# Two groups of weight parts, an earlier modulation region and moved down blocks in a hybrid backbone block

## The chip, the cores and the metric

The kernel runs on one core of a Trainium2 chip. A core has a matrix engine (TensorE, "PE" in the profile, with its weight loads as "PEld"), a vector engine (DVE), a scalar engine (ACT), GpSimd (POOL), and SyncE (SP), which here only issues DMAs. TensorE writes to eight accumulation banks (PSUM); everything else works on the on-chip memory (SBUF). The metric is the device time of one execution in microseconds (us); lower is better.

## The reference, cut to what matters

One layer of a backbone for 512 latent tokens (8 rows of 64) and 256 context tokens, model width 2048, all in f32. First a mixer, then an MLP:

```python
mod = (c_act @ w_mod + b_mod)
sh1, sc1, gt1, sh2, sc2, gt2 = jnp.split(mod, 6, axis=-1)
h = rmsnorm(x, g_norm1) * (1 + sc1) + sh1
...                                   # 4 GLA heads and 4 mLSTM heads, both directions
x = x + gt1 * merge_groups(...)       # gates, per-head norm, output projection w_out
h2 = rmsnorm(x, g_norm2) * (1 + sc2) + sh2
x = x + gt2 * conv_ffn(h2, rows, GRID_W, w_up, conv_w, conv_b, w_down)
return rmsnorm(x, g_final)

def conv_ffn(h, rows, cols, w_up, conv_w, conv_b, w_down):
    u = h @ w_up
    u_gate, u_val = jnp.split(u, 2, axis=-1)            # 5504 columns each
    g = conv3x3_depthwise(u_gate on the 8 x 64 grid) + conv_b
    return (jax.nn.silu(g) * u_val) @ w_down
```

The six modulation regions sh1 to gt2 each are 2048 sums over 2048 inputs. The last one, gt2 (region 5), scales the MLP's output.

## The kernel before, in words

Activations lie transposed, features on the 128 partitions and tokens along the free axis. Each f32 matmul is made of three in a faster 32-bit format (`fp32r`): an operand is split in a high part (a cast on ACT, line 91) and a low part (the difference, on DVE, line 92), and `mm3` (L106) adds high x high, high x low, low x high. So every weight block goes through DMA to a `raw` buffer, an ACT cast to `hi` and a DVE subtraction to `lo`, in `load_split` (L176). The pools of these three are in `wts`.

Order of work: head projections (`project_steps`, L357), woven into the scans of the head before; gates (`w_gates`), output projection (`w_out`), second norm, then the MLP in 11 units of features: unit 0 has 3 blocks of 128 features, the ten others 4 each (43 in all). A unit is: gate half of the up-projection (`up_gate`, tiles `ug`), 3x3 convolution on ACT and DVE (`convolve`), value half (`up_val`, tiles `uv`), products `gh`/`gl`, and the down-projection in four blocks of 512 outputs (`down_sums`, tiles `dn`), which in the program stand one unit later, between the gate half and the value half of the next unit. Their results go from the banks through ACT to `st` tiles and by POOL's accumulating DMAs to `dacc` in HBM (units 0 to 8) or, scaled by region 5, to `x2d` (later ones). `fold` (L1265) scales `dacc` once and adds it to `x2d`, in unit 9.

The up-projections of units 1 to 10 use a 2 x 2 block scheme with seven products (`seven`, L1153) in place of eight: of a weight block of 512 columns and a token block of two k-rows, quarter sums are formed. The token sums are made once (`token_sums`, `token_last`, tiles `bq` and `bt`). The weight sums are made on DVE for every block by `load_sums` (L186): a `raw` tile of 7 x 256 columns takes the 4 loaded quarters and 3 sums written beside and over them, and then all 1792 columns are cast and subtracted as one part. `four` (L1165) combines the seven banks.

Modulation regions 2 to 5 are no matmuls: a chunk (`mod_chunk`, L283) loads 512 KB of `w_mod` and adds two scaled halves to a sum tile on DVE; 8 chunks make a quarter of a region, then four small matmuls with ones and one more on TensorE end it (`mod_sums`, `mod_end`; TensorE keeps these in written order). Chunks are a list of "fillers"; each `load_split` or `load_sums` calls `fill`, which takes `rate[0]` of them on average. Before: regions 2, 3, 4 fill the mLSTM heads' projections (rate 2 from the fourth step on), the gates and the output projection (rate 1.5); region 5 fills the down blocks of units 0 to 7 (rate 0.7), and its chunks take their buffers from the MLP's own `raw` pool (three buffers). In the heads, a chunk's buffer is one of the scan's tiles `sc` and `qi`.

A planner at build time orders the instructions of each engine and gives out buffers: by program order, with blocks in `high_priority` first, and with an instruction held back while its buffer is still in use by a modelled time. Where `pinned` is set, TensorE keeps the written order. A tile pool with tags gives each tag its own buffers; `yp` has sixteen 128 x 512 tiles, `y0` to `y15` (`ytile`), which hold x, then the MLP's convolutions and products. Before the MLP the banks are two pools, `psA` (six, tag `acc`) and `psB` (two); `st_p.close()` (L1114) ends them and one pool of eight takes their place. The broadcast of the second norm's statistics is in a bank of `psB`, read by L1109 for all 16 blocks of x.

Of the kernel before, what the change touches and what calls it, by code (L numbers as in the profile page):

```python
# [18 lines left out]
P = 128  # L19
# [52 lines left out]
def block_kernel(ctx: ExitStack, tc: tile.TileContext, a: dict, out: bass.AP):  # L72
# [102 lines left out]

    def load_split(src, name, n=2, w=512):  # L176
        raw = wts[0].tile([P, n, w], F32, name=f"raw_{name}", tag="raw")
        hi = wts[1].tile([P, n, w], F32R, name=f"hi_{name}", tag="hi")
        lo = wts[2].tile([P, n, w], F32R, name=f"lo_{name}", tag="lo")
        nc.sync.dma_start(raw, src)  # L180
        with tc.high_priority():
            parted[0] = split(hi, lo, raw)
        fill()
        return hi, lo

    def load_sums(src, name):  # L186

        x = wts[0].tile([P, 7, HW], F32, name=f"raw_{name}", tag="raw")
        hi = wts[1].tile([P, 7, HW], F32R, name=f"hi_{name}", tag="hi")
        lo = wts[2].tile([P, 7, HW], F32R, name=f"lo_{name}", tag="lo")  # L190
        nc.sync.dma_start(x[:, 0:4, :], src.rearrange("p a (b c) -> p (a b) c", c=HW))
        with tc.high_priority():
            add(x[:, 4:6, :], x[:, 0:4:3, :], x[:, 1:2, :].to_broadcast([P, 2, HW]))
            add(x[:, 6, :], x[:, 5, :], x[:, 0, :])
            add(x[:, 1, :], x[:, 2, :], x[:, 6, :])
            split(hi, lo, x)
        fill()
        return hi, lo
# [747 lines left out]
    mod_fillers((2, 3, 4))  # L946
# [60 lines left out]
    rate[0] = 1.5  # L1007
# [74 lines left out]
    pinned[0] = False  # L1082
    assert not fillers
# [5 lines left out]
    wts[:] = [pool(ctx, "mraw", 3, waits="tile"), pool(ctx, "mhi", 2, waits="tile"), pool(ctx, "mlo", 2, waits="tile")]  # L1089
# [3 lines left out]
    mod_raw.append(wts[0])  # L1093
    rate[0] = 0

# [17 lines left out]

    st_p.close()  # L1114
    banks8.append(pool(ctx, "psM", 8, PSUM, waits="tile"))
# [29 lines left out]
    def sum_tile(i, name):  # L1145
        return ytile(15, f"sum{i}_{name}") if i else fp.tile([P, T], F32, name=f"sum{i}_{name}", tag="sum0")


    mod_fillers((5,))

    PRODUCTS = ((0, bq, 0), (2, bq, 2), (6, bt, 2), (4, bt, 1), (5, bt, 0), (1, bq, 3), (3, bq, 1))

    def seven(src, name):  # L1153

        ps = [acc(f"{name}_{n}", (P, 2, HW)) for n in range(7)]
        for kp in range(KP):
            wh, wl = load_sums(src[kp], f"{name}_{kp}")
# [278 lines left out]
```

## Time and profile before

| | |
|---|---|
| median of 3 runs | 2653.06 us (2650.87 to 2656.63) |
| profiled execution | 2654.82 us, its span 2653.1 us |
| TensorE busy | 2513.1 us (95%), mean granted clock 0.984 |
| DVE, ACT, POOL busy | 68%, 37%, 8% |
| data moved | 380.56 MB, mean 143 GB/s |
| gates and output projection | about 762 to 1138 us of the span |
| MLP, units 0 to 10 | about 1146 to 2644 us |

Times in the trace are in us from the span's start. A line of a group or of the timeline has the program line, the engine, the operation, `out<-in` by tile names, shapes, the count, then the time; in brackets or behind a bar stands how long the engine had been idle just before, and what ended that idle time. A line of a stretch has its bounds and length, then busy time (and count) of PE, PEld, DVE, ACT and POOL, the granted TensorE clock as a share of full speed, the mean busy share of the 16 DMA engines and GB/s. Matmuls overlap their successors, so the step from one to the next is shorter than a matmul's own time.

### The profile page before, as it was taken

The numbers are of one execution on the slowest core, as the hardware profiler recorded it, in microseconds if no ns is written. First come the engines' busy times: TensorE is split into PE (matmuls) and PEld (weight loads), VectorE is DVE, ScalarE is ACT, GpSimd is POOL, SyncE is SP. The second block draws the span as 40 slices with busy tenths as digits, with TensorE's granted clock in tenths as the row PEclk, the third lists the DMA queues.
The fourth block names the chain that finished last, engine by engine and source line by source line (L and its number), as shares of the span: only waits on it lengthen the run. The fifth ranks groups of instructions, "written<-read, shape, count | busy, mean of one in ns | idle before, by whom it ended". The sixth has DMA issues, their size and how long they took to land.

```text
span 2653.1 us, 38849 instructions
## 1 busy us (share of the span) xinstructions
PE 2513.1 (95%) x15740; PEld 2230.2 (84%) x15740; DVE 1805.1 (68%) x2720; ACT 993.5 (37%) x1370; POOL 200.3 (8%) x274
## 2 busy tenths in 40 slices
PE   6999999999999999979998999999999999997997
PEld 4887899898888888868897989797988898987886
DVE  6657655454457576378887777777787777774866
ACT  4225543322222332254434343333433334343434
POOL 0000000000000000000102020101010101013021
PEclk9999999999999999989999999999999999999999
DMA  9740011132256686223537373736373645469473
GB/s 380 273 144 31 27 49 48 64 127 90 89 180 220 213 277 218 98 70 108 187 104 184 98 180 99 177 110 168 118 183 110 162 121 140 118 142 205 126 198 103
DMA packets 124108, 380.56 MB, mean 143 GB/s; under 512 B 14420, under 2 KB 18840, under 8 KB 123928
## 3 DMA queue, kind: packets, MB, share of 16 engines
q1 hardware_dynamic: 94680, 318.29, 35.9%
q0 software_dynamic: 28160, 58.73, 12.1%
q8 instruction: 123, 2.02, 0.3%
q10 hardware_dynamic: 1088, 1.05, 0.1%
q14 instruction: 57, 0.47, 0.1%
HBM read 323.49 MB, written 54.53 MB: 142 GB/s over the span
## 4 chain that ended last, share of the span: by engine, by line
PE 67%; DVE 14%; DMA 10%; issue 7%; POOL 1%; ACT 1%; SPq 0%; DVEq 0%; POOLq 0%; ACTq 0%
PE a L97 18%; PE uv L97 12%; PE ug L97 10%; PE ga L97 7%; PE wo L97 7%; PE dn L97 4%; DMA raw_m<-in_w_mod 4%; PE po L97 3%; DMA raw_uv<-in_w_up 3%; DVE cv L1208 2%; DVE lo_ug L92 2%; DVE lo_d L92 2%; DVE raw_ug L88 1%; PE sl L97 1%; PE ps_m L97 1%
## 5 line engine op out<-in xcount | busy, mean ns | idle before, releaser
L97 PE MATMUL dn<-gh,lo_d 128*128 128x512 f32 x672 | 266.0, 396 | 19.8 <-DVE lo_d L92 19.7
L97 PE MATMUL dn<-gh,hi_d 128*128 128x512 f32 x672 | 265.1, 395 | 5.1 <-ACT gh L91 5.1
L97 PE MATMUL dn<-gl,hi_d 128*128 128x512 f32 x672 | 264.4, 393 | 0.0
L1208 DVE SCALAR_TENSOR_TENSOR cv<-pads,cwt,cv 128x512 f32<-128x512 f32 x344 | 240.1, 749 | 2.2 <-ACT cv L1206 1.6
L97 PE MATMUL uv<-bqh,lo_uv 128*128 128x256 f32 (+1 forms) x688 | 205.1, 299 | 32.8 <-DVE lo_uv L92 32.7
L92 DVE TENSOR_TENSOR lo_uv<-raw_uv,hi_uv 128x1792 fp32r<-128x1792 f32 (+1 forms) x88 | 169.2, 1926 | 96.6 <-ACT hi_uv L91 96.5
L97 PE MATMUL ug<-bqh,hi_ug 128*128 128x256 f32 (+1 forms) x688 | 201.1, 296 | 31.5 <-DVE x L1109 17.8
L91 ACT CAST hi_uv<-raw_uv 128x1792 fp32r<-128x1792 f32 (+1 forms) x88 | 141.7, 1610 | 233.0 <-PE uv L97 198.2
L92 DVE TENSOR_TENSOR lo_ug<-raw_ug,hi_ug 128x1792 fp32r<-128x1792 f32 (+1 forms) x88 | 168.7, 1925 | 74.2 <-ACT hi_ug L91 74.1
L97 PE MATMUL uv<-bqh,hi_uv 128*128 128x256 f32 (+1 forms) x688 | 203.2, 295 | 6.6 <-ACT hi_uv L91 6.6
L91 ACT CAST hi_ug<-raw_ug 128x1792 fp32r<-128x1792 f32 (+1 forms) x88 | 140.9, 1612 | 169.3 <-PE ug L97 110.9
L97 PE MATMUL uv<-bql,hi_uv 128*128 128x256 f32 (+1 forms) x688 | 202.7, 295 | 0.0
L97 PE MATMUL ug<-bqh,lo_ug 128*128 128x256 f32 (+1 forms) x688 | 197.8, 298 | 5.0 <-DVE lo_ug L92 4.9
L298 DVE SCALAR_TENSOR_TENSOR sum_m<-raw_m,csil,sum_m 128x512 f32<-128x512 f32 x240 | 180.0, 750 | 31.4 <-DMA raw_m<-in_w_mod 26.8
L97 PE MATMUL ug<-bql,hi_ug 128*128 128x256 f32 (+1 forms) x688 | 197.9, 291 | 0.0
L88 DVE TENSOR_TENSOR raw_uv<-raw_uv 128x256 f32<-128x256 f32 (+1 forms) x240 | 121.7, 512 | 96.8 <-DMA raw_uv<-in_w_up 93.2
L1263 POOL DMA_DIRECT2D dacc<-st x128 | 111.9, 923 | 964.8 <-ACT st L1259 964.3
L97 PEld LDWEIGHTS dn<-gh,lo_d 128*128 128x128 f32 x672 | 127.7, 190 | 52.9 <-DVE lo_d L92 26.5
L97 PEld LDWEIGHTS uv<-bqh,lo_uv 128*128 128x128 f32 x688 | 134.5, 196 | 38.1 <-DVE lo_uv L92 36.2
L97 PEld LDWEIGHTS ug<-bqh,hi_ug 128*128 128x128 f32 x688 | 132.5, 193 | 37.6 <-issue 21.6
L97 PEld LDWEIGHTS dn<-gh,hi_d 128*128 128x128 f32 x672 | 127.7, 190 | 31.7 <-ACT gh L91 5.3
L97 PE MATMUL a<-hi_h,hTh 128*128 128x256 f32 x512 | 150.5, 294 | 0.5 <-ACT e L391 0.5
(349 smaller groups left out, 6811.6 us busy)
## 6 DMA issues: line engine op xcount, KB each, us to landing
raw_m<-in_w_mod SPq DMA_DIRECT2D x192, 512.0 KB, 5.0
raw_d<-in_w_down SPq DMA_DIRECT2D x82, 512.0 KB, 3.8
raw_ug<-in_w_up SPq DMA_DIRECT2D x80, 512.0 KB, 3.5
raw_uv<-in_w_up SPq DMA_DIRECT2D x80, 512.0 KB, 5.3
dacc<-st POOLq DMA_DIRECT2D x144, 256.0 KB, 5.5
raw_h<-in_w_heads SPq DMA_DIRECT2D x64, 512.0 KB, 3.5
raw_ga<-in_w_gates SPq DMA_DIRECT2D x32, 512.0 KB, 3.5
raw_wo<-in_w_out SPq DMA_DIRECT2D x32, 512.0 KB, 3.6
```

What stands on the lines that cost most here:

```text
L88: V.tensor_tensor(out=o, in0=x, in1=y, op=ALU.add)
L91: S.copy(hi, x)
L92: return V.tensor_tensor(out=lo, in0=x, in1=hi.bitcast(F32), op=ALU.subtract).ins
L97: ins = PE.matmul(*args, **kw)
L298: V.scalar_tensor_tensor(out=parts[0], in0=x, scalar=ck, in1=parts[0], op0=ALU.mult, op1=ALU.add)
L1208: V.scalar_tensor_tensor(out=t3, in0=src, scalar=w, in1=t3, op0=ALU.mult, op1=ALU.add)
L1263: nc.gpsimd.dma_start(x2d[k] if q > FOLD else dacc[k], t, accum_op=ALU.add)
```

## The change

Four things are edited.

1. `load_sums` no longer makes one part of seven quarters. The host orders each block's quarters as 0, 2, 3, 1. The first three are split as they are, in buffers of their own (`ahi`, `alo`, two each); three additions on DVE write four sums to a separate tile (`msum`, two), which is split in the buffers that down weights use too (`mhi`, `mlo`, two each). `raw` has four buffers of 4 KB a partition instead of three of 7 KB. The seven products are reordered so that the three plain ones come first, and `four` follows.
2. Region 5 joins regions 2 to 4 ahead of the MLP. Head 4's projection, woven into the last GLA head's scan, gets fillers as well (10 chunks), and the rate in gates and output projection goes from 1.5 to 2. The MLP has none.
3. The gate half of unit 0 is traced ahead of `st_p.close()`, so it accumulates in `psA`.
4. Unit 0: token sums of pairs 7 to 3 go ahead of the value half, the others and `token_last` behind it; its tiles take other places in `yp`; two of its down blocks go ahead of unit 1, the first of them feature by feature. The fourth down block of unit 9 goes behind the value half of unit 10, the last four blocks of x are fetched later, and some tiles of the end change places.

```diff
+    def split_new(x, name, shape, at=1):
+        hi = wts[at].tile([P, *shape], F32R, name=f"hi_{name}", tag=f"hi{at}")
+        lo = wts[at + 1].tile([P, *shape], F32R, name=f"lo_{name}", tag=f"lo{at}")
+        parted[0] = split(hi, lo, x)
+        return hi, lo
...
     def load_sums(src, name):
-        x = wts[0].tile([P, 7, HW], F32, name=f"raw_{name}", tag="raw")
-        hi = wts[1].tile([P, 7, HW], F32R, name=f"hi_{name}", tag="hi")
-        lo = wts[2].tile([P, 7, HW], F32R, name=f"lo_{name}", tag="lo")
-        nc.sync.dma_start(x[:, 0:4, :], src.rearrange("p a (b c) -> p (a b) c", c=HW))
+        x = load_raw(src, name).rearrange("p a (b c) -> p (a b) c", c=HW)
+        s = wts[5].tile([P, 4, HW], F32, name=f"sum_{name}", tag="sum")
         with tc.high_priority():
-            add(x[:, 4:6, :], x[:, 0:4:3, :], x[:, 1:2, :].to_broadcast([P, 2, HW]))
-            add(x[:, 6, :], x[:, 5, :], x[:, 0, :])
-            add(x[:, 1, :], x[:, 2, :], x[:, 6, :])
-            split(hi, lo, x)
-        fill()
-        return hi, lo
+            plain = split_new(x[:, 0:3, :], f"a{name}", (3, HW), 3)
+            add(s[:, 0:2, :], x[:, 0:3:2, :], x[:, 3:4, :].to_broadcast([P, 2, HW]))
+            add(s[:, 2, :], s[:, 1, :], x[:, 0, :])
+            add(s[:, 3, :], s[:, 2, :], x[:, 1, :])
+            sums = split_new(s, f"b{name}", (4, HW))
+        return plain, sums
...
-            rate[0] = 2 if h > H and kp >= 3 else 0
+            rate[0] = 2 if h >= H and kp >= 3 else 0
...
-    mod_fillers((2, 3, 4))
+    mod_fillers((2, 3, 4, 5))
...
-    rate[0] = 1.5
+    rate[0] = 2.0
...
-    wts[:] = [pool(ctx, "mraw", 3, waits="tile"), pool(ctx, "mhi", 2, waits="tile"), pool(ctx, "mlo", 2, waits="tile")]
+    wts[:] = [pool(ctx, n, b, waits="tile")
+              for n, b in (("mraw", 4), ("mhi", 2), ("mlo", 2), ("ahi", 2), ("alo", 2), ("msum", 2))]
...
-    st_p.close()
-    banks8.append(pool(ctx, "psM", 8, PSUM, waits="tile"))
...
-    mod_fillers((5,))
-    PRODUCTS = ((0, bq, 0), (2, bq, 2), (6, bt, 2), (4, bt, 1), (5, bt, 0), (1, bq, 3), (3, bq, 1))
+    PRODUCTS = ((0, 0, bq, 0), (0, 1, bq, 2), (0, 2, bq, 1), (1, 2, bt, 2), (1, 0, bt, 1), (1, 1, bt, 0), (1, 3, bq, 3))
...
+            put(1, 0, v, p4, ALU.subtract)
             put(1, 1, v, p5, ALU.add)
             sub(u, u, p5)
             put(0, 1, u, p3, ALU.add)
-            put(1, 0, v, p4, ALU.subtract)
...
-            t = ytile(8 + 2 * i, f"cv{f}")
+            t = ytile(8 + i if q == 0 else 8 + 2 * i, f"cv{f}")
...
-    for q in range(NQ):
+    up_gate(0)
+    st_p.close()
+    banks8.append(pool(ctx, "psM", 8, PSUM, waits="tile"))
+    for j in reversed(range(3, KP)):
+        token_sums(j)
+    up_val(0, convolve(0))
+    for j in range(3):
+        token_sums(j)
+    for j in range(KP):
+        token_last(j)
+    down_sums(0, (0, 1), True)
+    for q in range(1, NQ):
         up_gate(q)
-        if q == 0:
-            for j in range(KP):
-                token_sums(j)
-        if q:
-            rate[0] = 0.7 if q < FOLD + 1 else 0
-            down_sums(q - 1)
-            rate[0] = 0
+        down_sums(q - 1, (2, 3) if q == 1 else range(3) if q == NQ - 1 else range(4))
         if q - 1 == FOLD:
             fold()
         up_val(q, convolve(q))
-        if q == 0:
-            with tc.high_priority():
-                for j in range(KP):
-                    token_last(j)
+    down_sums(NQ - 2, (3,))
...
-    for k in range(KT):
+    for k in range(12):
         nc.gpsimd.dma_start(x2[k], x2d[k])
...
+        if blk == 0:
+            for k in range(12, KT):
+                nc.gpsimd.dma_start(x2[k], x2d[k])
...
+    r["w_up4"] = up.reshape(20, KP, P, 4, HW)[:, :, :, [0, 2, 3, 1], :].reshape(up.shape)
```

More of the change, by code (lines that the diff above doesn't have):

```diff
@@ L1082, in block_kernel @@
     pinned[0] = False
+    print("LEFT", len(fillers))
     assert not fillers
@@ L1265, in fold @@
     def fold():
-        assert not fillers
         for k in range(KT):
@@ L1305, in tile @@
             n = self.at.setdefault(tag, len(self.at))
-            if n < 8:
-                return ytile(8 + n, name, shape, dtype)
-            return operand((n - 8) % 4 + 4, "hl"[(n - 8) // 4], "t", name, shape, dtype)
+            return ytile((n + 8) % 16, name, shape, dtype)
     sqp = Late()
```

57 lines of the change are left out of this document (31 added, 26 removed).

## The prediction

> **What bounds the kernel now.** I read the page's busy lines first, then the chain that ended last, then busy time by stretches cut at the ends of the up products, then TensorE's own waits, and last the single instructions behind the terms below.
>
> ```profile
> PE 2513.1 (95%) x15740; PEld 2230.2 (84%) x15740; DVE 1805.1 (68%) x2720; ACT 993.5 (37%) x1370; POOL 200.3 (8%) x274
> ...
> PE 67%; DVE 14%; DMA 10%; issue 7%; POOL 1%; ACT 1%; SPq 0%; DVEq 0%; POOLq 0%; ACTq 0%
> ```
>
> TensorE is the bound, but only two thirds of the chain is matmul; DVE and DMA hold 24%. The next table (stretch, then busy time and count per engine, granted clock, DMA share, GB/s) says where. Rows are: two for head groups 3 to 5, gates and output projection in two parts, the passage to the MLP, unit 0, unit 1, and then periods from one `uv` end to the next (the first and last of six with modulation in them, one nearly without, the one with the fold, the last).
>
> ```profile
> 403.00:485.00 82.00, 80.36 (x500) 74.34 (x498) 39.88 (x64) 28.36 (x60) 1.47 (x2) 1.00 0.18 59
> 485.00:565.00 80.00, 79.99 (x463) 67.69 (x464) 45.21 (x95) 24.24 (x49) 3.15 (x8) 1.00 0.20 65
> ```
> ```profile
> 832.00:1060.00 228.00, 228.00 (x1045) 186.58 (x1045) 151.00 (x197) 66.51 (x85) 4.51 (x8) 1.00 0.70 241
> 1060.00:1138.30 78.30, 78.09 (x359) 63.61 (x357) 29.24 (x37) 18.31 (x22) 3.65 (x7) 1.00 0.31 104
> ```
> ```profile
> 1138.30:1164.60 26.30, 8.32 (x55) 7.82 (x55) 22.39 (x37) 21.18 (x34) 0.68 (x2) 0.64 0.15 50
> 1164.60:1232.10 67.50, 67.47 (x287) 55.66 (x288) 57.36 (x106) 33.76 (x54) 0.00 (x0) 0.96 0.27 88
> 1232.10:1354.20 122.10, 116.83 (x817) 109.92 (x816) 97.62 (x129) 49.03 (x52) 8.65 (x16) 0.97 0.46 151
> 1354.20:1494.70 140.50, 131.11 (x874) 121.21 (x873) 105.61 (x142) 52.74 (x55) 14.02 (x16) 0.96 0.53 139
> ...
> 2037.50:2171.00 133.50, 128.05 (x868) 118.20 (x867) 104.57 (x140) 52.41 (x54) 14.01 (x16) 0.99 0.55 142
> 2171.00:2303.00 132.00, 126.76 (x876) 117.20 (x875) 99.26 (x133) 53.27 (x55) 13.91 (x16) 1.00 0.51 128
> 2303.00:2450.90 147.90, 131.29 (x866) 121.01 (x864) 96.50 (x129) 62.50 (x69) 36.05 (x47) 0.97 0.70 164
> 2450.90:2590.10 139.20, 128.08 (x865) 118.60 (x865) 104.36 (x138) 56.67 (x59) 23.79 (x34) 0.99 0.63 165
> ```
>
> Gates and output projection leave TensorE no hole at DMA share 0.70. The MLP does. Its unhindered matmul steps come from two pieces of the chain (start, length, count):
>
> ```profile
> 870.97 21.89 PE ga L97 x96
> ...
> 2469.55 28.88 PE ug L97 x238
> ```
>
> 21.89/96 = 0.228 us for 512 columns, 28.88/238 = 0.121 us for 256. A period has 336 + 336 small and 192 large matmuls: 672 x 0.1205 + 192 x 0.2275 = 124.7 us. It takes 132.0 to 140.5, 147.9 with the fold. TensorE's waits between 1354 and 2171 us (total, times, longest), and those of DVE in the same stretch:
>
> ```profile
> PE uv L97 <- DVE lo_uv L92: 20.2, 8, 4.6
> PE dn L97 <- DVE lo_d L92: 15.2, 9, 3.2
> PE ug L97 <- ACT hi_ug L91: 5.5, 6, 0.9
> ...
> DVE raw_uv L88 <- DMA raw_uv<-in_w_up: 49.8, 24, 7.9
> ...
> DVE sum_m L298 <- DMA raw_m<-in_w_mod: 23.0, 10, 4.8
> ```
>
> So TensorE waits for DVE's low parts, and DVE, in order, had stood at additions or modulation sums whose data had not landed. Weights of `uv` land later than those of `ug` (KB each, median us from issue to landing), as they are fetched while the down stage stores and the modulation loads:
>
> ```profile
> raw_ug<-in_w_up SPq DMA_DIRECT2D x80, 512.0 KB, 3.5
> raw_uv<-in_w_up SPq DMA_DIRECT2D x80, 512.0 KB, 5.3
> ```
>
> **Passage to the MLP and unit 0.** The first unit's second matmul waits for the last reader of the broadcast statistics:
>
> ```profile
> 1146.33 0.47 PE L97 MATMUL ug<-bqh,hi_ug 128*128 128x512 f32 x1
> ...
> 1164.63 2.47 PE L97 MATMUL ug<-bqh,hi_ug 128*128 128x512 f32 x5 [17.82 <-DVE x L1109]
> 1166.90 2.76 PE L97 MATMUL ug<-bqh,lo_ug 128*128 128x512 f32 x6
> 1169.46 1.60 PE L97 MATMUL ug<-bql,hi_ug 128*128 128x512 f32 x6
> ```
>
> Its own operand was there at 1146.33; L1109 reads the broadcast bank, and a bank of the new eight lies on it. Old banks end that wait. Next to be late are the operands. From the trace's groups by shape (count, busy, mean ns):
>
> ```profile
> L1208 DVE SCALAR_TENSOR_TENSOR cv<-pads,cwt,cv 128x512 f32<-128x512 f32 x344 | 240.1, 749 | 2.2 <-ACT cv L1206 1.6
> L298 DVE SCALAR_TENSOR_TENSOR sum_m<-raw_m,csil,sum_m 128x512 f32<-128x512 f32 x240 | 180.0, 750 | 31.4 <-DMA raw_m<-in_w_mod 26.8
> L92 DVE TENSOR_TENSOR lo_uv<-raw_uv,hi_uv 128x1792 fp32r<-128x1792 f32 x80 | 161.6, 2023 | 93.0 <-ACT hi_uv L91 92.9
> ...
> L92 DVE TENSOR_TENSOR lo_d<-raw_d,hi_d 128x1024 fp32r<-128x1024 f32 x82 | 100.2, 1222 | 25.5 <-ACT hi_d L91 25.4
> ...
> L88 DVE TENSOR_TENSOR raw_ug<-raw_ug 128x256 f32<-128x256 f32 x160 | 67.7, 423 | 2.9
> ...
> L88 DVE TENSOR_TENSOR raw_ug<-raw_ug 128x512 f32<-128x512 f32 x80 | 55.0, 688 | 13.6 <-DMA raw_ug<-in_w_up 13.0
> ...
> L1111 DVE SCALAR_TENSOR_TENSOR bql<-x,mod,bqh 128x512 fp32r<-128x512 f32 x16 | 11.1, 747 | 0.0
> ```
> ```profile
> 1142.36 0.96 DVE L92 TENSOR_TENSOR lo_ug<-raw_ug,hi_ug 128x768 fp32r<-128x768 f32 x1 [0.16 <-ACT hi_ug L91]
> ...
> 1146.58 2.06 DVE L1109 SCALAR_TENSOR_TENSOR x<-x,mod,rb_rms 128x512 f32<-128x512 f32 x3
> ```
>
> Back to back an operand pass is 2.06/3 = 0.69 us. A pair of operand tiles costs DVE 4 x 0.69 + 0.96 = 3.7 us against 18 x 0.228 = 4.1 of TensorE, so matmuls can follow them, some 2 us late. To the end of unit 1 TensorE then needs 8.0 (1138.3 to 1146.3) + 2 + 3 x 32.8 (two gate/value units of 144 large matmuls and all of down 0) + 2 x 40.5 = 189 us. DVE from 1144.4: modulated operands 32 x 0.69 = 22; low parts of unit 0, 15 x 0.96 = 14; token differences 8 x 2.8 + 8 x 0.42 = 26; convolutions 24 + 32 taps x 0.75 = 42; unit 0's products 6 x 0.69 = 4; down 0's parts 4 x (1.22 + 0.69) = 8; the two sevens 16 x (0.69 + 0.85 + 0.96 + 1.22) = 60; their combinations 12: 188 us. Ends, if neither ever waits: 1327 and 1332. Moving half of down 0 ahead of unit 1 gives DVE 16 us of cover before unit 1, and takes that cover from convolution 1. Two engines so evenly loaded don't overlap wholly; I add 7 us: 1339 against 1354.2, **15 us less** (ends 0 and 27).
>
> [...] The row: after the 17.8 us wait, eleven matmuls took 4.8 us (1164.63 to 1169.46) where 11 x 0.228 is 2.5, and the clock granted in the stretch of the wait was 0.64. [...]
>
> **Units 2 to 9, up to the fold (1354.2 to 2345.7).** Ideal: 8 x 40.5 + 7 x 84.2 = 913; taken 991.5: 78 us of holes.
>
> Modulation leaves: 32 chunks of 512 KB and 2 DVE passes (48 us of DVE in all), which shared the three raw buffers, and the wait of their sums. The period nearly without them has 132.0 - 124.7 = 7.3 us of holes; at that rate 8 units lose 58.
>
> The split: one part of 1792 columns becomes 768 + 1024. DVE pays 0.96 + 1.22 - 2.02 = 0.16 us more per step, 16 steps: 2.5 us a period; DVE at 99.3 + 2.5 stays under 124.7. Three of seven products need no addition; their buffers are apart from the down weights, so they are ready before `uv` starts; the raw buffer is freed once added up, not once split, and there are four. That attacks the landing wait and the `lo_uv` start. What stays: combinations crowding DVE at the start of `ug` and `lo_d`. I take 3 us a unit, nearer to 0 than to 7.3 as two of the three largest waits lose their cause: 24 instead of 78, **54 us less** (ends 20, if the split gives nothing, and 78).
>
> **Fold and end.** The fold is not touched:
>
> ```profile
> ACT fold L1271 <- DMA fold<-dacc: 35.3, 14, 6.5
> ```
>
> ACT's casts queue behind these waits (2390 to 2451 us); deeper loads don't pass them. I take 4 us (ends -5 and +20). At the end
>
> ```profile
> L97 PE MATMUL dn<-gh,hi_d 128*128 128x512 f32 x672 | 265.1, 395 | 5.1 <-ACT gh L91 5.1
> ```
>
> one wait of 5.1 us follows the last `uv`; the block moved there (48 x 0.228 = 10.9 us) covers it. With 1 us of that `uv`'s own start, part of the mean wait of 20.2/8 = 2.5 above, that is **6 us** (ends 0 and 8). Its stores precede the last four loads of x, 25 us ahead of their use.
>
> **Where the modulation goes.** Ten chunks join head 4, where DVE has 85.1 of 162 us busy; their buffers come free with the last GLA outputs, and behind a waiting chunk on SP stand head weights, four buffers deep. Issues of two neighbouring steps, just after:
>
> ```profile
> 568.20 0.33 SPq L180 DMA_DIRECT2D raw_h<-in_w_heads  x1
> ...
> 575.92 0.33 SPq L180 DMA_DIRECT2D raw_h<-in_w_heads  x1
> ```
>
> At 7.7 us a step three spare buffers are 23 us of cover. Some 22 come to gates and output projection (2 for 1.5 a step, less those served earlier): 22 x 1.5 = 33 us of DVE on 180 in 306, and 11.5 MB, which lifts 206 GB/s to 243; 241 was held from 832 to 1060 without a hole. If DVE were full there, it would cost up to 33. Their last sums now come near the end of the stage, in TensorE's written order: **2 us more** (ends 0 and 10).
>
> Sum: 15 + 54 + 4 + 6 - 2 = 77. The profiled execution took 2654.8 us (span 2653.1), 0.07% over the median of three, 2653.06, so nothing is corrected: 2654.8 - 77 = 2578.
>
> **Rivals.** Rival 1. The split gives nothing; only modulation goes. The same 7.3 us hole in a period without modulation speaks for it, the shared buffers against. With 12 at the passage and nothing at the fold: 2654.8 - (12 + 20 + 6 - 2) = 2619.
>
> Rival 2. Deeper loading also takes the fold's holes and the passage overlaps fully: 2654.8 - (27 + 54 + 20 + 6 - 2) = 2550. Against it: the fold's casts are late through ACT's order, not through loads.
>
> Rival 3. Slower: two handoffs ACT to DVE to TensorE per step in place of one, in queues that keep their order. One exposed wait of 0.9 us (5.5/6 above) in each of 160 steps is 147 us: 2725. It decides from 77/160 = 0.48 us a step. For it: casts already stand behind waits in the fold. Against: a steady step has 42 x 0.1205 = 5.06 us of matmul and 0.69 + 0.85 + 2.18 = 3.7 of DVE. [...]
>
> Rival 4. The planner fits unit 0 badly, as convolution tiles now need the last token differences: their 26 us stand in series instead of 15 won, and the units win 30 in place of 54: 2654.8 + 26 - 30 - 4 - 6 + 2 = 2643.
>
> **How the numbers follow.** Forecast 0.55, rival 1 0.18, 2 0.08, 3 0.12, 4 0.07. Likeliest range of the forecast alone 2558 to 2600. The range 2548 to 2632 leaves out rivals 3 and 4 (0.19). Faster by over 0.2% (about what a measurement can tell here): 0.86; within it 0.02; slower 0.12.
>
> **What would show it.** The wait on L1109 gone and the first matmuls of unit 0 following at once; unit 1's `uv` ending near 1339; periods near 127.5 us with `lo_uv` waits under 1 us; DMA share about 0.7 up to the end of the output projection with TensorE still full; the fold's period still over 140. Wrong if periods stay at 132 (rival 1), if every step shows a wait for the plain or the summed parts (rival 3), or if holes open between 403 and 1138 us.

## The result, and the profile after

| | before | after |
|---|---|---|
| median | 2651.97 us (2647.62 to 2656.63) | 2571.22 us (2568.50 to 2575.02) |
| profiled execution, its span | 2654.82, 2653.1 us | 2568.50, 2566.8 us |
| ratio of after to before | | 0.9696, 95% interval 0.9675 to 0.9718 |

The change makes the kernel 81 us faster by the medians. The forecast was 2578 us, 77 us less than the profiled execution. The page of the kernel after, busy time per engine:

```profile
PE 2487.4 (97%) x15740; PEld 2218.3 (86%) x15740; DVE 1816.0 (71%) x2880; ACT 1021.1 (40%) x1530; POOL 200.5 (8%) x274
```

TensorE is busy for 97% of a shorter span; DVE's busy time barely moved (1805.1 to 1816.0 us), so the gain isn't work that went away. TensorE executes the same 15740 matmuls; its own busy time fell by 25.7 us, as matmuls behind a wait take longer steps (0.73 to 0.35 us in place of 0.227 behind one, shown below) and there are fewer waits. The busy time by stretches of the kernel after, with the columns of the prediction's table (length; busy time and count of PE, PEld, DVE, ACT, POOL; granted clock; DMA share; GB/s). First four stretches ahead of the MLP, then unit 0's gate half, its value half with half of down 0, unit 1, and then periods from one `uv` end to the next, the last row but two with the fold:

```profile
403.00:488.00 85.00, 83.35 (x513) 76.30 (x512) 43.49 (x70) 28.98 (x60) 1.47 (x2) 1.00 0.21 68
488.00:530.00 42.00, 36.47 (x220) 30.95 (x219) 33.10 (x51) 9.62 (x17) 0.00 (x0) 0.92 0.46 152
842.00:1060.00 218.00, 218.00 (x1014) 177.47 (x1013) 160.99 (x217) 63.03 (x82) 3.42 (x6) 1.00 0.79 276
1060.00:1150.90 90.90, 90.69 (x421) 73.65 (x420) 51.90 (x68) 22.52 (x29) 4.71 (x9) 1.00 0.51 177
1159.00:1193.20 34.20, 32.89 (x146) 26.91 (x145) 33.95 (x59) 30.17 (x49) 0.00 (x0) 1.00 0.26 81
1193.20:1255.60 62.40, 51.37 (x217) 41.52 (x218) 48.76 (x86) 28.97 (x49) 2.83 (x6) 0.92 0.34 112
1255.60:1352.90 97.30, 97.27 (x746) 94.06 (x745) 73.11 (x109) 42.76 (x54) 5.82 (x11) 1.00 0.39 131
1352.90:1482.70 129.80, 126.19 (x867) 117.18 (x866) 112.25 (x166) 56.95 (x72) 14.02 (x16) 1.00 0.50 130
1482.70:1607.00 124.30, 124.30 (x865) 116.66 (x865) 100.25 (x147) 55.31 (x70) 13.96 (x16) 1.00 0.54 136
...
2104.70:2229.10 124.40, 124.40 (x867) 116.76 (x866) 100.24 (x147) 55.42 (x70) 13.96 (x16) 1.00 0.54 136
2229.10:2372.10 143.00, 131.75 (x866) 122.55 (x865) 95.66 (x140) 61.98 (x82) 34.69 (x45) 0.94 0.69 166
2372.10:2496.10 124.00, 115.91 (x818) 109.46 (x817) 98.27 (x145) 53.18 (x67) 19.61 (x28) 0.97 0.60 158
2496.10:2566.80 70.70, 60.52 (x330) 52.26 (x328) 48.40 (x102) 37.05 (x70) 13.04 (x18) 0.96 0.43 127
```

The seven periods from unit 1's `uv` on took 135.5 us each on the mean before (1354.2 to 2303.0). Now the first takes 129.8, and six take 124.3 to 124.6: that is the ideal worked out from the step of a matmul, 124.7, with PE full but for 0.2 us in one of them. TensorE's waits between 1352.9 and 2310 us, all of them (total, times, longest):

```profile
PE ug L97 <- DVE u_uv L82: 1.6, 1, 1.6
PE ug L97 <- DVE t L1231: 1.1, 2, 0.9
PE ug L97 <- DVE lo_bug L92: 0.6, 1, 0.6
PE ug L97 <- ACT hi_bug L91: 0.3, 1, 0.3
```

Before, the three largest waits of a shorter stretch (1354 to 2171 us) came to 40.9 us. The wait on L1109 is gone as well; the first `ug` follows the idle products at once, but a new wait stands at the first down block. TensorE's timeline at these two places, start and length in us:

```profile
1156.91 2.30 PE L97 MATMUL idle<-sqsq,cst 128*128 128x128 f32 x14
1158.97 1.64 PE L97 MATMUL ug<-bqh,hi_ug 128*128 128x512 f32 x6
```
```profile
1240.17 0.80 PE L97 MATMUL dn<-gh,hi_d 128*128 128x512 f32 x1 [10.98 <-ACT gh L91]
1240.90 0.80 PE L97 MATMUL dn<-gl,hi_d 128*128 128x512 f32 x1
...
1243.20 0.51 PE L97 MATMUL dn<-gh,hi_d 128*128 128x512 f32 x1
1243.55 0.40 PE L97 MATMUL dn<-gl,hi_d 128*128 128x512 f32 x1
1243.78 0.39 PE L97 MATMUL dn<-gh,lo_d 128*128 128x512 f32 x1
```

Where the time went, by the starts of the matmuls that begin each stage (us; the last two columns are the difference and the prediction's term):

| stage | before | after | gained | predicted |
|---|---|---|---|---|
| start to the end of output projection | 1138.3 | 1150.9 | -12.6 | -2 |
| passage, units 0 and 1 | 216.0 | 202.0 | 14.0 | 15 |
| unit 2 to `ug` of unit 9 | 991.5 | 916.7 | 74.8 | 54 |
| fold: `dn` 8, `uv` 9, `ug` 10 | 152.5 | 153.5 | -1.0 | 4 |
| end: `dn` 9, `uv` 10, `dn` 10, last norm | 154.8 | 143.7 | 11.1 | 6 |
| sum | 2653.1 | 2566.8 | 86.3 | 77 |

That the sum came out near is partly luck: the terms missed in opposite senses. The modulation ahead of the MLP cost 10.6 us more and the fold gave 5 less, the units gave 20.8 us more and the end 5.1.

**Ahead of the MLP.** The new row 488 to 530 has TensorE at 36.47 of 42 us, its clock at 0.92 and DVE at 33.10. This is the end of head 4's projection, which now has modulation in it. TensorE's longest wait there, and DVE's timeline around its releaser:

```profile
PE pa L102 <- DVE cum L88: 3.9, 1, 3.9
```
```profile
513.55 0.94 DVE L88 TENSOR_TENSOR cum<-cum,pf 36x768 f32<-36x768 f32 x1
514.42 0.47 DVE L303 TENSOR_SCALAR sum_m<-raw_m,csil 128x512 f32<-128x512 f32 x1
514.81 0.41 DVE L864 TENSOR_SCALAR negg<-pf 4x512 f32<-4x512 f32 x1
515.15 0.73 DVE L305 SCALAR_TENSOR_TENSOR sum_m<-raw_m,csil,sum_m 128x512 f32<-128x512 f32 x1
515.81 0.21 DVE L866 TENSOR_SCALAR dg<-cst,pf 4x4 f32<-4x4 f32 x1
```

Between the small steps of the gate scan (`cum`, `negg`, `dg`) stand passes of 0.47 to 0.74 us for `sum_m`. The scan is a chain from one small step to the next, and TensorE waits for its end.

**The fold.** It is as it was. ACT's and TensorE's waits between 2310 and 2425 us:

```profile
ACT fold L1275 <- DMA fold<-dacc: 37.0, 11, 6.2
```
```profile
PE ug L97 <- DVE u_uv L82: 7.1, 1, 7.1
PE uv L97 <- ACT hi_buv L91: 6.4, 2, 3.9
PE uv L97 <- ACT hi_auv L91: 3.4, 1, 3.4
```

ACT waited 35.3 us for these loads before and 37.0 after, and its casts of weights stand behind them in its order.

### The profile page after: what moved, and what is told of

Its sections match the earlier page's. It is cut to its first block, busy times and chain, and to the rows that moved or that the text cites. A ratio compares the mean times of both kernels' runs of the same rounds, so it can differ in the third digit from the quotient of the medians.

```text
span 2566.8 us, 39444 instructions
## 1 busy us (share of the span) xinstructions
PE 2487.4 (97%) x15740; PEld 2218.3 (86%) x15740; DVE 1816.0 (71%) x2880; ACT 1021.1 (40%) x1530; POOL 200.5 (8%) x274
## 5 line engine op out<-in xcount | busy, mean ns | idle before, releaser
L97 PEld LDWEIGHTS dn<-gl,hi_d 128*128 128x128 f32 x672 | 126.5, 188 | 26.5 <-DVE gl L92 0.8
L97 PE MATMUL ug<-bth,hi_bug 128*128 128x256 f32 x480 | 137.3, 287 | 8.5 <-DVE u_uv L82 7.1
L97 PE MATMUL a<-lo_h,hTh 128*128 128x256 f32 x512 | 145.3, 284 | 0.0
L97 PE MATMUL a<-hi_h,hTl 128*128 128x256 f32 x512 | 145.2, 284 | 0.0
L97 PE MATMUL uv<-bth,hi_buv 128*128 128x256 f32 x480 | 137.8, 287 | 6.4 <-ACT hi_buv L91 6.4
L97 PE MATMUL uv<-bqh,hi_auv 128*128 128x256 f32 x480 | 136.7, 285 | 3.4 <-ACT hi_auv L91 3.4
L97 PE MATMUL uv<-bth,lo_buv 128*128 128x256 f32 x480 | 137.9, 287 | 1.2 <-DVE lo_buv L92 1.2
L97 PE MATMUL uv<-btl,hi_buv 128*128 128x256 f32 x480 | 137.4, 286 | 0.0
L97 PE MATMUL uv<-bqh,lo_auv 128*128 128x256 f32 x480 | 136.8, 285 | 0.2 <-DVE lo_auv L92 0.2
L97 PE MATMUL ug<-bqh,hi_aug 128*128 128x256 f32 x480 | 136.1, 284 | 0.7 <-DVE t L1231 0.4
```

What stands on the lines that cost most here:

```text
L97: ins = PE.matmul(*args, **kw)
```

## The experiments

The kernels were measured in three groups, each on a chip of its own and beside its own runs of the kernel before (medians 2660.09, 2656.14 and 2657.11 us), so across groups the ratios are what is compared; the kernel after has 0.9696 (0.9675 to 0.9718). Six kernels have intervals that overlap this one: region 5 back, three raw buffers, new banks, other tiles, block back and shared parts. What is read from these rests on their stages and waits, not on the ratio. This table gives the stages of each profiled run, cut as above, in us:

| kernel | ahead | passage | units 2 to 9 | fold | end | span |
|---|---|---|---|---|---|---|
| before | 1138.3 | 216.0 | 991.5 | 152.5 | 154.8 | 2653.1 |
| after | 1150.9 | 202.0 | 916.7 | 153.5 | 143.7 | 2566.8 |
| region 5 back in the MLP | 1139.7 | 202.6 | 940.5 | 156.6 | 143.7 | 2583.1 |
| region 5 moved, alone | 1151.8 | 210.3 | 960.4 | 154.2 | 156.7 | 2633.4 |
| one part | 1151.5 | 204.7 | 968.4 | 154.6 | 152.0 | 2631.3 |
| three raw buffers | 1153.3 | 200.3 | 918.4 | 159.2 | 143.7 | 2574.9 |
| first unit in new banks | 1153.2 | 207.0 | 916.6 | 158.7 | 143.6 | 2579.2 |
| nothing in head 4 | 1140.8 | 203.7 | 917.1 | 155.7 | 143.7 | 2560.9 |
| other tiles in unit 0 | 1151.4 | 210.6 | 919.1 | 154.7 | 143.7 | 2579.4 |
| no fold | 1150.6 | 207.0 | 916.8 | 124.4 | 144.1 | 2542.8 |
| no fold, nothing in head 4 | 1141.5 | 206.9 | 916.9 | 124.4 | 144.2 | 2533.8 |
| the same with early tiles | 1141.4 | 204.3 | 916.7 | 124.4 | 144.6 | 2531.4 |
| block of unit 9 back | 1152.5 | 203.5 | 916.5 | 157.2 | 153.2 | 2583.0 |
| shared parts | 1152.2 | 200.1 | 920.7 | 158.0 | 143.8 | 2574.9 |

Stages that a kernel doesn't edit show how far such numbers go: the fold, edited by none of the others, lies between 153.5 and 159.2 in the kernels with the split, the stretch ahead of the MLP between 1150.6 and 1153.3 where its modulation is as in the kernel after, and the passage between 200.1 and 203.7 where units 0 and 1 are as in the kernel after and the fold is there.

**Region 5 back in the MLP.** The kernel after, its last modulation region again among the down blocks:

```diff
-    mod_fillers((2, 3, 4, 5))
+    mod_fillers((2, 3, 4))
...
+    mod_fillers((5,))
...
-            rate[0] = 2 if h >= H and kp >= 3 else 0
+            rate[0] = 2 if h > H and kp >= 3 else 0
...
-    rate[0] = 2.0
+    rate[0] = 1.5
...
+        rate[0] = 0.7 if q < FOLD + 1 else 0
         down_sums(q - 1, (2, 3) if q == 1 else range(3) if q == NQ - 1 else range(4))
+        rate[0] = 0
```

Three raw buffers make room for it.

> The kernel after with modulation region 5 put back into the down blocks of the MLP (rate 0.7, no fillers in head 4, 1.5 in gates and output projection), its chunks taking the raw buffers of the weights, which are three here since the sum tiles need the space. The two groups of parts stay. Theory (the split closed most of the holes, modulation only some 20 us of them): the 12 us that region 5 cost ahead of the MLP come back, 20 to 30 us of holes return in units 1 to 8, about 2584 us. Rival (modulation sharing buffers and DVE was the cause of the holes, whatever the parts): 75 us of holes return, about 2634 us.

Measured: 2584.91 us (2580.72 to 2586.62), ratio 0.9718 (0.9689 to 0.9749). The stretch ahead of the MLP is back at 1139.7, and the units take 23.8 us more. (The second `mod_fillers` stands ahead of the MLP's products, the rates of 1.5 and 2.0 in gates and output projection.) TensorE's largest wait in them:

```profile
PE dn L97 <- DVE lo_d L92: 12.6, 11, 1.7
```

From unit 3 on the holes are in the down blocks alone, where the chunks are; `ug` and `uv` stay full. Only unit 2's `ug` is 2.3 us longer than in the kernel after. With the split, moving the region is worth 23.8 us in the units and costs 11.2 ahead of them.

**Region 5 moved, alone.** The kernel before with the same region moved ahead of the MLP in the same way, and nothing else.

```diff
-    mod_fillers((2, 3, 4))
+    mod_fillers((2, 3, 4, 5))
...
-            rate[0] = 2 if h > H and kp >= 3 else 0
+            rate[0] = 2 if h >= H and kp >= 3 else 0
...
-    rate[0] = 1.5
+    rate[0] = 2.0
...
-            rate[0] = 0.7 if q < FOLD + 1 else 0
+            rate[0] = 0
```

> The kernel before with region 5 moved ahead of the MLP and nothing else. Theory: 12 us lost ahead of the MLP, holes of units 2 to 9 fall from 78 to about 58 (7.3 a unit), net about 2644 us. Rival (modulation was the cause): the holes vanish as in the kernel after, about 2590 us.

Measured: 2634.97 us (2631.73 to 2636.81), ratio 0.9908 (0.9883 to 0.9934), 9 us below what was expected. It costs 13.5 us ahead of the MLP and gives 5.7 in the passage and 31.1 in the units, which keep 43.7 us of the holes that the kernel after doesn't have. With the run above, the 74.8 us of the units are 31.1 (region) + 43.7 (split), or 51.0 (split first) + 23.8: neither part gives the whole, and each is worth 7 us more when it comes first.

**One part.** The kernel after with weights and sums again as one part of 1792 columns, in two buffers each and three raw ones, the host's order and the products' order as before.

```diff
-        plain = split_new(x[:, 0:3, :], f"a{name}", (3, HW), 3)
-        add(s[:, 0:2, :], x[:, 0:3:2, :], x[:, 3:4, :].to_broadcast([P, 2, HW]))
...
-        sums = split_new(s, f"b{name}", (4, HW))
+        add(x[:, 4:6, :], x[:, 0:4:3, :], x[:, 1:2, :].to_broadcast([P, 2, HW]))
...
+        split(hi, lo, x)
```

> The kernel after with the seven quarters in one part of 1792 columns again (three raw buffers of seven quarters, adding in place, the old order of products and of the combination); region 5 stays ahead and all other edits stay. Theory: holes of about 6 to 7 us a unit return, 50 to 60 us, about 2625 us. Rival (modulation was the cause): no change, 2571 us.

Measured: 2637.28 us (2632.98 to 2638.68), ratio 0.9915 (0.9890 to 0.9941). The holes return in every unit, though no modulation is in them: 51.7 us in units 2 to 9, 8.3 at the end. TensorE's waits from 1352.9 to 2310 us:

```profile
PE ug L97 <- DVE t L1231: 11.4, 1, 11.4
PE uv L97 <- DVE lo_uv L92: 11.0, 7, 1.8
PE dn L97 <- DVE lo_d L92: 7.4, 5, 2.2
PE ug L97 <- ACT hi_ug L91: 6.8, 8, 1.0
```

The first is a single wait in unit 2's `ug`. The others are small and come back at fixed places: every `uv` waits at its third matmul (1.3 to 1.8 us), most `ug` at the third of their eight steps (0.9 us). All of TensorE's waits there come to 41 us, of the 55 us that these units take beyond the ideal; the rest is in longer steps. Beside them DVE's own wait for data, in this kernel and in the kernel after (total, times, longest in the same stretch):

```profile
DVE raw_uv L88 <- DMA raw_uv<-in_w_up: 89.1, 28, 5.8
```
```profile
DVE sum_uv L88 <- DMA raw_uv<-in_w_up: 14.7, 10, 2.3
```

The loads take as long in both, 5.3 us from issue to landing with one part and 5.2 in the kernel after. With one part they are issued later: in these units a load of `uv` is issued 17 us (median) ahead of the first matmul that uses it, and 26 us in the kernel after. What the issuing queue (SP) of the kernel with one part waited for most, and what that of the kernel after did (both from 1402 to 2310 us):

```profile
SPq L200 <- DVE lo_uv L92: 268.9, 56, 8.2
```
```profile
SPq L178 <- DVE lo_d L92: 309.4, 62, 8.0
SPq L178 <- DVE sum_uv L88: 245.7, 51, 12.7
SPq L178 <- DVE lo_aug L92: 148.3, 35, 4.9
```

With one part a raw buffer comes free with the last low part, with two when it has been added up and its plain quarters are split. This is one of the reasons that the prediction named. Around the start of unit 3's `uv` (its first matmul at 1585.81 us) the trace of the kernel with one part shows two effects, first on DVE, then on ACT:

```profile
1584.13 1.61 DVE L88 TENSOR_TENSOR raw_uv<-raw_uv 128x512 f32<-128x512 f32 x3 [2.74 <-DMA raw_uv<-in_w_up]
1585.66 3.95 DVE L92 TENSOR_TENSOR lo_uv<-raw_uv,hi_uv 128x1792 fp32r<-128x1792 f32 x2
```
```profile
1597.80 1.69 ACT L91 CAST hi_uv<-raw_uv 128x1792 fp32r<-128x1792 f32 x1 [3.39 <-PE uv L97]
```

At the start the first low part stands in DVE's order behind the additions of a later step, which waited for their load: there a load that is issued sooner would help. In the middle of the stage loads are not short: wherever the trace shows a landing, it is 11 us or more ahead of the first matmul that uses the load. There the cast waits until TensorE has done with the step before the last one, as the parts are two deep, and the low part is ready only 1.4 us (median) ahead of its first matmul. In the kernel after the low parts of `uv` are mostly ready 5.0 to 5.8 us ahead.

**Three raw buffers.** The kernel after, `("mraw", 4)` made `("mraw", 3)`.

> The kernel after with three raw buffers in place of four, all else as it is. Theory (early parts in buffers of their own, and sums in a tile of their own, close the holes): within 5 us of 2571. Rival (the fourth raw buffer, that is deeper loading, closes them): uv waits for landings again, 3 us or more a unit, above 2600 us.

Measured: 2572.39 us (2571.02 to 2576.57), ratio 0.9677 (0.9652 to 0.9702). No difference: the fourth raw buffer, which the prediction named among the reasons, does nothing that shows, though loads of `uv` are issued 20 us ahead of their first matmul in place of 26. DVE's wait for `raw_uv` is even 2.9 us in place of 14.7.

**Shared parts.** The kernel after, the three plain quarters split into the buffers of the sums and the down weights, four deep, with three raw buffers for room.

```diff
-              for n, b in (("mraw", 4), ("mhi", 2), ("mlo", 2), ("ahi", 2), ("alo", 2), ("msum", 2))]
+              for n, b in (("mraw", 3), ("mhi", 4), ("mlo", 4), ("ahi", 2), ("alo", 2), ("msum", 2))]
...
-            plain = split_new(x[:, 0:3, :], f"a{name}", (3, HW), 3)
+            plain = split_new(x[:, 0:3, :], f"a{name}", (3, HW))
```

> The kernel after with the three plain quarters split into the same buffers as the sums and the down weights, four high and four low parts deep instead of two and two (three raw buffers to make room, which alone changed nothing). If the gain of the split is its size and the earlier start, with as many buffers in all: about 2572 us. Rival (the gain is that the plain parts have buffers apart from the down weights): waits for low parts at the start of uv and in the down blocks return, some 2 to 5 us a unit, 2590 to 2615 us.

Measured: 2576.93 us (2575.76 to 2579.59), ratio 0.9695 (0.9672 to 0.9718). By the ratio it is the kernel after. TensorE has no wait at all between 1402.5 and 2310 us; the 4.0 us that the units take more are in unit 2's `ug`, beside 1.9 less in the passage. So it isn't the separate buffers of the plain part that close the holes, as the prediction had it. It is that a step comes in two parts. Which of its effects carries it (the raw buffer free before the sums are split, products that need no sum first, parts that come free sooner) no run separates; the trace of the kernel with one part shows the first at the start of `uv` and the last in its middle.

**Nothing in head 4.** The kernel after, the first ten chunks of modulation moved to gates and output projection.

```diff
-            rate[0] = 2 if h >= H and kp >= 3 else 0
+            rate[0] = 2 if h > H and kp >= 3 else 0
...
-    rate[0] = 2.0
+    rate[0] = 2.2
```

> The kernel after without fillers in head 4's projection, at rate 2.2 in gates and output projection instead. Theory (7 to 8 of the 12.6 us lost ahead of the MLP come from modulation sums put between the gate scans on DVE in head 4): about 2564 us, and the waits for the running sums near 514 us go. Rival (the 12.6 us are the price of the modulation wherever it stands, or DMA at over 0.8 share starves the gates): 2571 us or more.

Measured: 2564.04 us (2562.64 to 2566.94), ratio 0.9655 (0.9638 to 0.9672). Output projection ends at 1140.8 in place of 1150.9. Its stretches:

```profile
488.00:530.00 42.00, 42.00 (x260) 35.77 (x258) 23.85 (x37) 14.98 (x29) 3.15 (x8) 1.00 0.20 63
832.00:1060.00 228.00, 228.00 (x1064) 185.28 (x1063) 180.77 (x244) 66.20 (x87) 4.51 (x8) 1.00 0.84 292
```

Head 4 is full again, and the later stretch takes the ten chunks without a hole, DVE at 180.77 of 228 us. So 10.1 of the 12.6 us were the place of ten chunks, not the number of chunks ahead of the MLP.

**First unit in new banks.** The kernel after, unit 0's gate half behind the opening of the eight-bank pool.

```diff
-    up_gate(0)
     st_p.close()
     banks8.append(pool(ctx, "psM", 8, PSUM, waits="tile"))
+    up_gate(0)
```

> The kernel after with the gate half of unit 0 traced behind the opening of the eight-bank pool again. Theory (the 17.8 us wait was for the bank of the broadcast statistics, and DVE and TensorE are about equally loaded up to the end of unit 1): the wait for the last L1109 returns at the first unit, but DVE works on through it, and the hole in the first down block shrinks, so the total loses less than 17.8 us: about 2580 us. Rival (the wait is the whole term): 2589 us. If the bank was not the cause, 2571 us and no wait.

Measured: 2579.05 us (2578.04 to 2580.93), ratio 0.9709 (0.9694 to 0.9723). TensorE's wait is back,

```profile
PE ug L97 <- DVE x L1114: 16.7, 1, 16.7
```

but the wait of 11 us for `gh` isn't there any more, and the passage is only 5.0 us longer. DVE's work is the same, and it is what both waits wait for: with the first taken away, most of it comes back as the second.

**Other tiles in unit 0.** The second convolution of unit 0 stands in `y9`, which holds one of the token sums that `token_last` still reads. Here convolutions and products get other tiles:

```diff
-            t = ytile(8 + i if q == 0 else 8 + 2 * i, f"cv{f}")
+            t = ytile(8 + 2 * i, f"cv{f}")
...
-(ytile((11, 12, 13, 14, 15, 7)[2 * i + n]
+(ytile((11, 9, 13, 14, 15, 7)[2 * i + n]
```

> The kernel after with unit 0's three convolutions in y8, y10, y12 (free after the token sums) in place of y8, y9, y10 (y9 waits for the last token differences), its products in y11, y9, y13, y14, y15, y7. Theory (the 11 us hole in the first down block of unit 0 is the second convolution, held back by its tile): the hole falls to 3 us or less, about 2563 us. Rival (DVE is the bound of this stretch, so the order does not matter): the hole moves to the start of unit 1, 2571 us.

Measured: 2581.79 us (2581.10 to 2583.10), ratio 0.9719 (0.9704 to 0.9733): 6 us slower by the ratio (its interval overlaps that of the kernel after), 11 by the medians, where 8 us less had been expected. This theory fell in the form in which it was put. TensorE's wait for `gh`, and the stretch up to its end:

```profile
1237.10 0.79 PE L97 MATMUL dn<-gh,hi_d 128*128 128x512 f32 x1 [10.61 <-ACT gh L91]
```
```profile
1193.50:1237.10 43.60, 32.94 (x145) 26.95 (x145) 42.92 (x80) 21.66 (x37) 0.00 (x0) 0.92 0.32 96
```

The wait is as long, now ahead of the first feature's product in place of the second's: the products' odd tiles hold such sums as well, and the casts of `gh` waited for the last token difference. So the wait for a tile was moved, not taken away. DVE is busy for 42.92 of 43.60 us.

**No fold.** The kernel after, every down block scaled on ACT by region 5, which is there from the start of the MLP now, and added to `x2d` at once.

```diff
-                    S.activation(t, accs[i], AF.Copy, scale=modc[5][:, k : k + 1] if q > FOLD else 1.0)
-                    if q == 0:
-                        nc.gpsimd.dma_start(dacc[k], t)
-                    else:
-                        nc.gpsimd.dma_start(x2d[k] if q > FOLD else dacc[k], t, accum_op=ALU.add)
+                    S.activation(t, accs[i], AF.Copy, scale=modc[5][:, k : k + 1])
+                    nc.gpsimd.dma_start(x2d[k], t, accum_op=ALU.add)
...
-        if q - 1 == FOLD:
-            fold()
```

> The kernel after without the fold: as region 5 is known before the MLP, every down block is scaled on ACT and added to x2d directly. Theory (the 29 us of holes in unit 9's value half and unit 10's gate half are ACT's casts standing behind fold tiles that wait for DMA): both halves fall to 40.5 us, about 2543 us; the scaled evictions cost ACT 0.09 us more each, hidden. Rival (the accumulating stores and the loads of that stretch are the bound): 10 us or more of the holes stay, above 2553 us.

Measured: 2544.49 us (2543.69 to 2544.81), ratio 0.9577 (0.9563 to 0.9592). The period that held the fold:

```profile
2229.00:2353.00 124.00, 124.00 (x863) 116.36 (x863) 100.27 (x146) 56.87 (x70) 13.98 (x16) 1.00 0.56 136
```

It is as full as its neighbours. The fold was all of that stage's holes: 29.1 us. The run leaves out the fold's loads, scalings and stores together; that the loads do it, through ACT's order, is read from the waits above and wasn't separated. The span falls by 24.0 us only, since the passage is 5.0 us longer here. A new wait of TensorE in it, 2.3 us for an `st` tile, is part of that; the rest is open.

**No fold and nothing in head 4**, the two edits above together.

> Two edits of the kernel after together: head 4 without modulation chunks (its chunks go to gates and output projection at rate 2.2) and no fold (every down block scaled by region 5 on ACT and added to x2d). If the two losses lie apart in time, as the stages say, they add: 2571 - 7 (alone 2564) - 27 (alone 2544) = 2537 us. Rival: without the fold the late units become tight elsewhere, or the later chunks crowd the MLP's start, and the pair gives no more than the second alone, 2544 us.

Measured: 2535.20 us (2534.20 to 2535.87), ratio 0.9536 (0.9517 to 0.9554). They add: 1141.5 ahead of the MLP and 124.4 at the fold stand in one run.

**The same with early tiles.** The last kernel with other tiles for unit 0: the three convolutions and the first product take tiles that are free as soon as their token sums are made, the second and third take odd ones (`y11` and `y15` for their high parts), which aren't.

```diff
-            t = ytile(8 + i if q == 0 else 8 + 2 * i, f"cv{f}")
+            t = ytile(8 + 2 * i, f"cv{f}")
...
-(ytile((11, 12, 13, 14, 15, 7)[2 * i + n]
+(ytile((14, 6, 11, 13, 15, 7)[2 * i + n]
```

> The run of the two edits, with unit 0's tiles changed: convolutions in y8, y10, y12, the first products in y14 and y6, all of them tiles that are free once their token sums are made, so that neither convolution 2 nor the first product waits for the last token differences. Theory (DVE is the bound of that stretch, 42.92 of 43.6 us busy, so tiles only move the wait): within 4 us of that run, about 2537 us. Rival (the hole of 11 us is a matter of tiles): 8 to 11 us less, about 2528 us.

Measured: 2533.26 us (2532.63 to 2533.85), ratio 0.9529 (0.9511 to 0.9547). TensorE's largest wait in units 0 and 1, without and with early tiles:

```profile
PE dn L97 <- ACT gh L91: 11.3, 1, 11.3
```
```profile
PE dn L97 <- ACT gh L91: 8.7, 1, 8.7
```

2.6 us of the wait go, and 2.6 us of the passage (206.9 to 204.3), within the 4 us that were expected. But the trace doesn't show the reason that was given, DVE as the bound. The wait ends with the casts of the second and third product, and these waited for a tile that the last token differences (`bql`) still read:

```profile
1225.23 2.76 DVE L92 TENSOR_TENSOR bql<-x,bqh 128x256 fp32r<-128x256 f32 x8
```
```profile
1227.35 1.34 ACT L91 CAST gh<-cv 128x512 fp32r<-128x512 f32 x2 [4.38 <-DVE bql L92]
```

Ahead of `bql`, from 1219.55 us, DVE had put 4.7 us of additions and low parts of unit 1's weights, which nothing needs before unit 1. The kernel after has the same 4.7 us ahead of the last taps of its second convolution. So tiles for these two products that are free early, or another order on DVE, stand untested as cures. The ratios can't tell the two kernels apart; their ranges of times don't overlap. This kernel and the one without its tiles are faster than both that were compared.

**Block of unit 9 back.** The kernel after, the fourth down block of unit 9 ahead of unit 10's value half again.

```diff
-        down_sums(q - 1, (2, 3) if q == 1 else range(3) if q == NQ - 1 else range(4))
+        down_sums(q - 1, (2, 3) if q == 1 else range(4))
...
-    down_sums(NQ - 2, (3,))
```

> The kernel after with unit 9's fourth down block back ahead of unit 10's value half. Theory (the moved block covers the wait for gh that was 5.1 us before): that wait is back behind the last uv, 2576 us. Rival (the end was shortened by the split alone, the planner hides the wait otherwise): 2571 us.

Measured: 2585.00 us (2583.25 to 2586.35), ratio 0.9723 (0.9704 to 0.9742). The wait is back, longer than before:

```profile
PE dn L97 <- ACT gh L91: 7.6, 1, 7.6
```

The end stage takes 153.2 us in place of 143.7: 9.5 us for one block, of which 7.6 are this wait and 1.8 the slower steps of the matmuls behind it. What the span lost beyond that (6.7 us) lies in stages that weren't edited. By the ratio the loss is 7 us, with overlapping intervals.

## Why the prediction was right, and where it wasn't

**Passage, 15 predicted, 14.0 measured.** The step held: the L1109 wait went, and DVE's work became what is late next. The end at 1339 was missed, 1352.9, nearly all of it because the MLP began 12.6 us later. Three things in the step weren't seen. Half of down 0 ahead of unit 1 gave little cover, since it waited itself for `gh` (10.98 us), and the old banks alone were worth much less than the wait that they removed: 5.0 us of the passage for 16.7 us of waiting. The 188 us of DVE against 189 of TensorE in the prediction said as much. And the sum of DVE's work says nothing of its order: 4.7 us of unit 1's weights stood ahead of what the first products needed.

After that hole come seven matmuls at steps of 0.73 to 0.35 us in place of 0.227; from 1240.17 to 1243.78 eight steps take 3.61 us where 1.82 would do, 1.8 us lost, at a granted clock of 0.55 (0.92 for the whole stretch). In the first unit of the kernel before, the eleven matmuls behind the wait of 17.8 us took 4.8 us in place of 2.5, 2.3 us lost. The 1.8 us are the low end of what the runs show: at the same place the kernel with other tiles has 6.4 us of long steps behind a wait of 10.6 us and loses 3.2 us, and three raw buffers lose 3.1 behind 8.1.

**Units 2 to 9, 54 predicted, 74.8 measured.** Both causes were right, both sizes were too small. The prediction took 20 us for the modulation (78 less 58) and 34 for the split (58 less the 24 it left). Measured in the order that the prediction took them in, they are 31.1 and 43.7. Of the 78 us before, TensorE's waits are 51 and the rest is in longer steps; both are gone. The 3 us of holes that it left in each unit aren't there; 3.6 us are, in all eight, mostly at unit 2. "Combinations crowding DVE at the start of `ug` and `lo_d`" was the mis-sized step. In the kernel after the plain low part is ready 5.8 us ahead of the first matmul of a `ug` and 18.4 us ahead of that of a `uv` (medians); that this cover takes in the combinations is likely, but no run shows it. Of the reasons given for the split, the separate buffers (shared parts: ratio 0.9695) and the fourth raw buffer (0.9677) count for nothing that shows. The raw buffer that comes free sooner shows at the start of `uv` alone; in the middle of a stage it is the parts, which the prediction didn't name, that come free too late in the kernel with one part. The late landing of `uv` weights, which the prediction put down to stores and modulation, isn't the modulation's: it is 5.2 us in the kernel after, where the MLP has none.

**Fold, 4 predicted, -1.0 measured**, inside its range. The sentence that deeper loads don't pass ACT's casts was right (ACT waited 37.0 us for the fold's loads, 35.3 before) and should have made the term zero.

**End, 6 predicted, 11.1 measured**, beyond the bound of 8. The two parts of the sum came about as priced: the wait of 5.1 us went, and `uv` 10 itself took 1.9 us less where 1 was counted (with the wait, that stage went from 47.3 to 40.3 us). What the sum put at nothing are the steps behind the wait: in the kernel before they are long for 6.3 us after it (granted clock 0.61 from 2590.05 to 2598 us), which cost about 3 us. The down blocks of unit 9 gave 0.9 more. Neither edit does it alone: with the block moved but one part the end is 2.8 us shorter than before, with the split but the block in its old place 1.6 us, with both 11.1.

**Modulation ahead of the MLP, 2 predicted, 12.6 measured**, beyond the bound of 10. The step that failed is "ten chunks join head 4, where DVE has 85.1 of 162 us busy". It looked for a DVE that is full and for buffers that come free late. The cost was the order on DVE: passes of up to 0.75 us between the steps of a short chain on which TensorE waits, in 42 us of the 162. The share over 162 us didn't show those 42. Without these chunks the stretch takes 1140.8, 2.5 us over before, about the 2 that were predicted for all of them; what is left is for the chunks that went to gates and output projection.

**The rivals.** A split that gives nothing (2619) is ruled out by the kernel with one part, which loses 51.7 us of the units again. The slower rival, two handoffs in place of one, would have shown waits for the plain or summed parts in every step; all such waits of units 2 to 9 come to 0.9 us. The planner's bad fit came true as a hole of 11 us, not 26. The forecast and the deeper rival (2550) were mixed: the units did better than the forecast, and the fold gave nothing, nearer to the forecast's 4 us than to that rival's 20.

## What to carry to other kernels

Where a weight step is loaded, summed, cast and subtracted as one block, cut it in two: DVE is busy for longer (11 us here), and TensorE loses its holes (43.7 us here in units 2 to 9). The traces suggest why, though no run separates it: each part's buffer comes free sooner, and so does the raw one, so the low parts of `uv` are mostly ready 5.0 to 5.8 us ahead in place of 1.4. Put filler passes where the engine's order has no chain of short steps that another engine waits for (ten chunks in such a chain were 10.1 us here); judge that in windows as short as the chain, not by the mean share of a stage. And when a wait is taken away, look at what the engine behind it does meanwhile: if it is full, or has work in its order that could come later, the wait can come back later (here 11.0 us at the first down block for 16.7 us at the first `ug`). Where both a wait and the long steps behind it go, count both (5.1 and about 3 us here).

## What was not expected of the hardware

DMA didn't slow TensorE even at a high rate: in the kernel with nothing in head 4, 292 GB/s at a share of 0.84 over 228 us left TensorE no hole (228.00 of 228.00 us, clock 1.00). And how long a load takes said little about the whole: `raw_uv` took 5.2 us to land in the kernel after and 3.6 with three raw buffers, and the two kernels' times can't be told apart.

How long TensorE's steps stay long behind a wait doesn't follow the wait's length in these traces: 3.38 us behind 10.98 us (kernel after, 1240.17 to 1243.55 us), 6.3 behind 5.05 (the end of the kernel before), 4.8 behind 17.8 (its first unit).
